# Two-operand head work on VectorE, score copies and a scale on ScalarE, and a later first weight load in a decoder trunk on one NeuronCore

## The chip, the core and the metric

The kernel runs on one core of a Trainium2 chip. A core has five engines with queues of their own: TensorE (PE, with a separate queue for weight loads, PEld), VectorE (DVE), ScalarE (ACT), GpSimd (POOL) and SyncE (SP), which here only issues DMAs. The metric is device time of one execution in microseconds, the median over runs; lower is better.

## The reference

One layer of a hybrid decoder on 1024 tokens of width 1024, with 16 learned tokens put in front, all in float32:

```
u = rmsnorm(h, mix_norm_pre)
q, f_logit, i_in, g_out, v_pool, gate_a, gate_b = split(u @ w_in)      # 512 x5, 1024 x2
a = hgrn2(q, f_logit, i_in, g_out, lb, out_norm)      # 4 heads of 128 x 128
p = multiscale_pool(v_pool, pool_proj, pool_scale)    # windows 2, 4, 8, 16
z = sigmoid(gate_a) * (a @ w_branch_hgrn) + sigmoid(gate_b) * (p @ w_branch_pool)
h = h + rmsnorm(z @ w_out, mix_norm_post)
u = rmsnorm(h, ffn_norm_pre)
y = (gelu(causal_dwconv(u @ ffn_w_gate)) * (u @ ffn_w_up)) @ ffn_w_down   # width 2816
h = h + rmsnorm(y, ffn_norm_post)
```

The part that the change works in is `hgrn2`, a linear recurrence with a decay per token and channel:

```
f     = lb + (1 - lb) * sigmoid(f_logit)
log_f = log(max(f, 1e-30))
k     = (1 - lb) * sigmoid(-f_logit)
state = exp(log_f) * state + k v^T ;  o = q state
o     = rmsnorm(o per head) * out_gain * sigmoid(g)
```

## The kernel before

*Stages.* The kernel goes once through these stages, with 128 channels on the partitions and all tokens along the free axis: norms of the input rows and the V projection (to about 80 us), the first output gates G0 and G1 and the branch gates (to about 260), the head stage (260 to 480), the two branch projections (480 to 560), the mixing with w_out (560 to 700), the FFN's gate and up projections (700 to 1115) and its down projection (to the end). Every weight tile is split for two-term arithmetic: ACT casts it to `whi`, and another engine subtracts, `wlo = wraw - whi` (L155).

*The start.* `load_row` loads one of nine tiles of input rows (L454). Their loads are written first, then four weight tiles (`wiraw`, L459) and small parameters (`prow`, L478). The first loads of the output gate's weights, `gl` (a `Loader`, whose `wsplit` has its load at L151), are written far later, inside the loop over V tiles. PE begins with warm-up matmuls (L507, `pj`) until the first normalised row is there to be transposed (L431, `pt<-ident,un`).

*The head stage.* The order of projections (F: forget gate, Q, G: output gate, PV and PP: pooling) and of the four heads' steps (`h0` to `h3`, `c0` to `c3`) is written out by hand in `ORDER`. After an F projection, `post_f` takes two sigmoids of it, `f` and `kk`, and `chain_f` (the `c` steps) makes from them the scaled `kk`, the logarithm of the decay in two pieces (`f2` and `f`, two ACT logarithms), their sum (L636) and its running sum `b` (L637). `head_steps` then makes the scores within chunks of 128 tokens in levels of 2, 4, 8, 16, 32 and 64 tokens. `level_in` makes for each level the differences `d` from `b` (L684), two exponentials on ACT (L686, L687), and the products with `q` (L688) and `kk` (L689). `level_mm` multiplies these on PE into a bank `sl` (L699 for the levels 32 and 64, L705 for the small ones). `level_out` brings the bank into `sc` by copies (L714, levels 32 and 64) or into `near` by masked copies (L720). Then come the decayed `kd` and `qs`, transposes of `kd` into `kt` (L763), the diagonal products of `kk` and `q` (`kk` scaled by `e1` at L755, matmuls L773 into `sb`, copies L777 into `sc`), the state (`ds`, L790), the output `o`, its square `rs` (L814), the split of that for a mean by matmul (L872, `rh`), and the norm (L821, L822). A projection's matmuls are L208 to L212, its banks `pg` for G, `pq` for Q.

*Who does what.* Names of operations such as `lq64.0` (level 64's product with `q`, head 0) go through this function:

```
    def eng(op):
        return pool_e if op in POOLED else dve
```

`POOLED` names 44 operations: 31 of the heads' two-operand operations (with one split of `rs`), and 13 (`w...`) subtractions of weight splits.

*What sets the order.* PE, ACT and DVE run in the written order at the start and in parts of the stages after it, under `tc.manual_schedule`; elsewhere the framework's scheduler orders each engine's instructions, by its own estimates and by when buffers come free. SP's DMAs are ordered by it everywhere.

Of the kernel before, what the change touches and what calls it, by code (L numbers as in the profile page):

```python
# [11 lines left out]
AF = mybir.ActivationFunctionType  # L12
ALU = mybir.AluOpType

P = 128
# [19 lines left out]
NCH = 8  # L35
# [4 lines left out]
LOG_FLOOR = 1e-30  # L40
LSPLIT = 2.0 ** -60
LUP = 2.0 ** 60
# [6 lines left out]
EARLY_G = 2  # L49
# [12 lines left out]
POOLED = ("e1k.0 e1k.3 kdmul.2 kdmul.3 kdsub.2 lk32.1 lk4.1 lq16.1 lq32.1 lq32.2 lq64.0 lq64.3 lq8.0 lq8.1 lq8.2 "  # L62
          "osg.2 sub2.2 sub32.1 sub8.1 wBA2 wBA6 wBA7 wBB2 wF0 wF2 wF3 wPP2 wPV0 wPV1 wQ0 wQ1 lq4.3 kdsub.1 qsmul.1 "
          "lk32.0 e1q.3 e1q.1 lq2.1 wQ2 sub2.3 rsl.0 lk32.3 lq64.1 qsmul.2").split()
TRUNC = False

CH_ALL = [(0, 348), (348, 346), (694, 346)]
# [4 lines left out]
def trunk_kernel(ctx: ExitStack, tc: tile.TileContext, x, meta_tokens, mix_norm_pre,  # L72
# [3 lines left out]
    nc = tc.nc  # L76
    act, dve, pool_e, pe = nc.scalar, nc.vector, nc.gpsimd, nc.tensor
# [24 lines left out]
    def slot(n, dtype=F32, name="s"):  # L102
        return stage["fm", "p"].tile([P, n], dtype, tag="fm", name=nm(name), padded_shape=[P, LP])
# [17 lines left out]
    def small(shape, name, tag, bufs=4):  # L121
        return sm.tile(shape, F32, tag=tag, name=nm(name), bufs=bufs)
# [328 lines left out]
    def load_row(t0, rows):  # L451
        row = slot(D, name="row")
        src = meta_tokens[:, :] if t0 == 0 else x[0, t0 - NM : t0 - NM + rows, :]
        nc.sync.dma_start(row[:rows], src)  # L454
        return row

    def load_wi(j):
        raw = slot(1024, name="wiraw")
        nc.sync.dma_start(raw.rearrange("p (k c) -> p k c", k=2), wblock(WIN, 2 * j, 2, CI, 512))  # L459
        return raw  # L460
# [24 lines left out]
    oml = const.tile([P, HEADS], F32, name="oml")  # L485
# [90 lines left out]
    SB = 32  # L576
# [39 lines left out]
    def eng(op):  # L616
        return pool_e if op in POOLED else dve

# [8 lines left out]

    def chain_f(h, kk, b, f, f2):
        dve.tensor_scalar(f, f, oml[:, h : h + 1], lb[:, h : h + 1], ALU.mult, ALU.add)
        dve.tensor_scalar(kk, kk, oml[:, h : h + 1], None, ALU.mult)  # L630
        dve.tensor_scalar(f2, f, LUP, 1.0, ALU.mult, ALU.min)
        dve.tensor_scalar(f2, f2, LOG_FLOOR * LUP, None, ALU.max)
        dve.tensor_scalar(f, f, LSPLIT, None, ALU.max)
        act.activation(f2, f2, AF.Ln)
        act.activation(f, f, AF.Ln)
        eng(f"lf.{h}").tensor_tensor(f, f, f2, ALU.add)  # L636
        dve.tensor_tensor_scan(b, keep_on, f, 0.0, ALU.mult, ALU.add)  # L637
        heads[h].update(kk=kk, b=b, f=f)
# [7 lines left out]
    def head_steps(h):  # L646
        q, kk, b, lf = (heads[h][z] for z in ("q", "kk", "b", "f"))
# [5 lines left out]
        sc = slot(NCH * P, name="sc")  # L653
        scm, em = small([NM, HALO], "scm", "scm", 2), small([P, HALO * NM], "em", "em", 2)
        near = small([P, NCH * SB], "near", "near", 2)
        n3 = near.rearrange("p (c t) -> p c t", c=NCH)
        pool_e.memset(sc, 0.0)
        pool_e.memset(near, 0.0)

        def over(t):  # L660
            return t[:, :NM].rearrange("p (o t) -> p o t", o=1).to_broadcast([P, HALO, NM])
# [46 lines left out]
        def level_out(lv, ps):  # L708
            if lv >= SB:
                o3 = sc.rearrange("p (c t) -> p c t", c=NCH)  # L710
                p3 = ps[:, : NCH * lv].rearrange("p (c h) -> p c h", c=NCH)
                for i in range(P // (2 * lv)):
                    n = 2 * lv * i
                    dve.tensor_copy(o3[n : n + lv, :, n + lv : n + 2 * lv], p3[n : n + lv])  # L714
                return
            o4 = near.rearrange("p (c b two h) -> p c b two h", c=NCH, two=2, h=lv)[:, :, :, 1, :]
            p4 = ps[:, : NCH * SB // 2].rearrange("p (c b h) -> p c b h", c=NCH, h=lv)
            nb = SB // (2 * lv)
            m4 = masks[lv].rearrange("p (o b h) -> p o b h", o=1, h=lv).to_broadcast([P, NCH, nb, lv])
            dve.copy_predicated(o4, m4, p4)  # L720
# [195 lines left out]
    def job(kind, i):  # L916
        if kind == "F":
            return (wblock(WIN, 0, KD, CF + i * P, P), KD, u_all, CH_ALL, lambda r: post_f(i, r))
        if kind == "Q":
            return (wblock(WIN, 0, KD, CQ + i * P, P), KD, u_q, CH_Q, lambda r: post_q(i, r))  # L920
        if kind == "G":
            return (wblock(WIN, 0, KD, CG + i * P, P), KD, u_q, CH_Q, lambda r: post_g(i, r))
        if kind == "PV":
            return (wblock(WIN, 0, KD, CV + i * P, P), KD, u_all, CH_ALL, lambda r: post_pv(i, r))
        if kind == "PP":
            return (pool_proj[0, i].rearrange("(k c) d -> c k d", k=1), 1,
                    lambda k, lo, n: (pin[i][0][:, lo : lo + n], pin[i][1][:, lo : lo + n]), CH_Q,
                    lambda r: post_pp(i, r))
        if kind == "BA":
            return (wblock(w_branch_hgrn[0], 0, HEADS, i * P, P), HEADS, a_x, CH_Q, lambda r: post_branch(sas, i, r))  # L930
        return (wblock(w_branch_pool[0], 0, HEADS, i * P, P), HEADS, p_x, CH_Q, lambda r: post_branch(sbs, i, r))
# [122 lines left out]
    with tc.manual_schedule(engines={E.Activation, E.DVE, E.PE}):  # L1054
        warm(14)
        n0, n1 = (norm_steps(rows_in[i], P, g1) for i in range(2))
        next(n0)
        next(n0)
        un0 = next(n0)
        f0 = feature_steps(un0, P, uhi, ulo, vtiles[0][0])  # L1060
        split_wi(raws[0])
        next(f0)
        next(f0)
        next(f0)
        next(n1)
        next(f0)
        next(n1)
        un1 = next(n1)
        v_mm(vb[0], vtiles[0][0], 0)
        v_mm(vb[0], vtiles[0][0], 1)  # L1070
        split_wi(raws[1])
        f1 = feature_steps(un1, P, uhi, ulo, vtiles[1][0])
        next(f1)
        next(f1)
        split_wi(raws[2])
        next(f1)
        next(f1)
        split_wi(raws[3])
        for i, j in ((0, 1), (1, 0), (0, 2), (1, 1), (0, 3), (1, 2), (1, 3)):
            for k in (2 * j, 2 * j + 1):  # L1080
                v_mm(vb[i], vtiles[i][0], k)
        v_norm(2)
        v_norm(3)
        for i in range(2):
            v_feat(2 + i)
            v_norm(4 + i)
        for i in range(2):
            v_out(vb[i], vtiles[i][0])
        for i in range(2, len(vtiles)):
            ps = bank("pv")  # L1090
            for k in range(KD):
                v_mm(ps, vtiles[i][0], k)
            if i < 5:
                v_feat(i + 2)
            if i == 5:
                v_feat(7)
                v_feat(8)
            v_norm(i + 4)
            if i == 3:
                params()  # L1100
            if i == 5:
                for q in ("t2", "t1", "t3", "t4"):
                    two_halves(gq, q)
                sums = [gate_steps(d) for d in ds]
            if i == len(vtiles) - 1:
                gl = Loader([job("G", h)[:2] + (P,) for h in range(EARLY_G)])
            for j in SUMS_AT.get(i, ()):
                next(sums[j], None)
            v_out(ps, vtiles[i][0])
        gates.load_first(0)  # L1110
        gates.load_first(1)
        gates.ahead(2)
        for h in range(EARLY_G):
            src, n_k, xs, chunks, post = job("G", h)
            r = proj(None, 0, n_k, xs, chunks, ws=gl.next(), name="pg", by_bank=2 * h)
            if h == EARLY_G - 1:
                post(r)
            for j in SUMS_AT.get(9 + 2 * h, ()):
                next(sums[j], None)
            if h < EARLY_G - 1:  # L1120
                post(r)
            if h == 0:
                dve.tensor_tensor(vm_hl[:NM], vm_hl[:NM], vm_low[:NM], ALU.add)
                nc.sync.dma_start(vmd, vm_hl[:NM])
                gates.load_first(2)
                gates.ahead(4)
            for j in SUMS_AT.get(10 + 2 * h, ()):
                next(sums[j], None)

        close_pool("ps")  # L1130
        open_pool("pf", 4, PSUM)
        gates.load_first(3)
        for e in range(0, EARLY, 2):
            p = gates.start_pair(e)
            for f in [f[i] for i in range(2) for f in p]:
                f()
                for j in SUMS_AT.get(13, ()) if e == 0 else ():
                    next(sums[j], None)
# [31 lines left out]
    for kind, i in order:  # L1170
# [18 lines left out]
        src, n_k, xs, chunks, post = job(kind, i)  # L1189
# [34 lines left out]
    for name, names in (("v1", ("b11h", "b11l", "b21h", "b21l")), ("v2", ("b22h", "b22l", "t1h", "t1l"))):  # L1224
        n, o = (HP, HO) if name == "v1" else (HN, 0)
# [113 lines left out]
    rows, z_at = {}, {}  # L1339
# [470 lines left out]
```

## Time and profile before

| | before |
|---|---|
| median of 3 runs | 1331.35 us (1329.1 to 1331.79) |
| the profiled execution's own time | 1331.5 us |
| its span | 1329.8 us |
| mean granted TensorE clock | 0.991 |
| PE busy | 1302.7 us, 98% |
| PEld busy | 1159.9 us, 87% |
| DVE busy | 968.0 us, 73% |
| ACT busy | 572.9 us, 43% |
| POOL busy | 438.5 us, 33% |
| DMA moved | 230.56 MB, 173 GB/s on average |

The span is the part of an execution that the profiler's records cover; the profiled execution's own time is 1.7 us longer. "Busy" counts the time in which an engine works on an instruction; "granted clock" is the share of full speed that TensorE was allowed. The records name instructions by line of the kernel (L154), by operation, and by output and inputs (`whi<-wraw`). Times are from one profiled execution.

### The profile page before, as it was taken

To read this page: it belongs to the slowest core of one execution; us is meant where nothing else is said; L and a number is where in the kernel's file an instruction comes from. 1 tells how busy PE (TensorE), PEld (TensorE's weight loads), DVE (VectorE), ACT (ScalarE), POOL (GpSimd) and SP (SyncE) were. 2 spreads that over 40 slices of the span, in tenths; PEclk is the share of its full clock that TensorE was granted. 3 is DMA by queue.
4 is the path that set the end of the run, shared out by engine and by line. 5 is a ranking of instruction groups with operands and counts; after the bars stand their busy time and mean duration, and the time that the engine had idled before them with its cause. 6 is when DMAs were issued, how large, how long until landed. Compare 5 with 4: busy or idle time off the path is not lost.

```text
span 1329.8 us, 21860 instructions
## 1 busy us (share of the span) xinstructions
PE 1302.7 (98%) x8665; PEld 1159.9 (87%) x8665; DVE 968.0 (73%) x1229; ACT 572.9 (43%) x962; POOL 438.5 (33%) x333
## 2 busy tenths in 40 slices
PE   8999999998899999999999999999999999999997
PEld 6799899998898999987899888888888888888886
DVE  5765655379967767766678999888999895455757
ACT  5553333366666665235564222322222233444443
POOL 2015331226624710051025555545555652000000
PEclk9999999998998999999999999999999999999999
DMA  7134533321011157987686777676766799666644
GB/s 260 53 105 145 134 111 104 108 69 49 19 52 36 35 175 263 337 287 253 229 291 231 192 207 193 196 206 164 181 157 141 183 237 318 216 224 222 222 174 158
DMA packets 139832, 230.56 MB, mean 173 GB/s; under 512 B 9080, under 2 KB 77340, under 8 KB 139730
## 3 DMA queue, kind: packets, MB, share of 16 engines
q1 hardware_dynamic: 127666, 204.78, 45.9%
q0 software_dynamic: 12064, 24.38, 11.1%
q8 instruction: 68, 1.11, 0.3%
q14 instruction: 34, 0.28, 0.1%
HBM read 165.59 MB, written 86.57 MB: 190 GB/s over the span
## 4 chain that ended last, share of the span: by engine, by line
PE 91%; DVE 3%; ACT 2%; DMA 2%; issue 1%; POOL 1%; SPq 0%; DVEq 0%; ACTq 0%
PE P L311 15%; PE P L312 15%; PE P L314 15%; PE pd L188 5%; PE pd L190 5%; PE pd L189 5%; PE pm L188 2%; PE pm L190 2%; PE pm L189 2%; PE ppv L208 1%; PE ppv L212 1%; PE ppv L209 1%; PE pbb L208 1%; PE pbb L209 1%; PE pbb L212 1%; PE pv L189 1%
## 5 line engine op out<-in xcount | busy, mean ns | idle before, releaser
L312 PE MATMUL P<-v,whi 128*128 128x512 f32 (+2 forms) x408 | 140.7, 353 | 0.0
L311 PE MATMUL P<-v,whi 128*128 128x512 f32 (+2 forms) x408 | 140.7, 352 | 0.0
L314 PE MATMUL P<-v,wlo 128*128 128x512 f32 (+2 forms) x424 | 135.1, 349 | 0.0
L1544 DVE TENSOR_TENSOR rot<-wraw,rot 128x1024 fp32r<-128x1024 f32 x31 | 37.9, 1224 | 72.3 <-ACT rot L1543 72.3
L282 POOL TENSOR_TENSOR swa<-wraw,wraw 128x512 f32<-128x512 f32 x28 | 43.4, 1549 | 138.9 <-DMA wraw<-in_ffn_w_gate_dram 73.9
L311 PEld LDWEIGHTS P<-v,whi 128*128 128x128 f32 x408 | 76.7, 188 | 10.5
L312 PEld LDWEIGHTS P<-v,whi 128*128 128x128 f32 x408 | 76.6, 188 | 10.2
L314 PEld LDWEIGHTS P<-v,wlo 128*128 128x128 f32 x424 | 74.0, 188 | 10.8
L256 ACT CAST whi<-wraw 128x512 fp32r<-128x512 f32 x78 | 46.1, 617 | 86.5 <-PE P L312 63.0
L190 PE MATMUL pd<-rot 128*128 128x512 f32 x272 | 82.1, 389 | 0.0
L189 PE MATMUL pd<-rot 128*128 128x512 f32 x272 | 82.1, 389 | 0.0
L188 PE MATMUL pd<-rot 128*128 128x512 f32 x272 | 81.1, 389 | 0.1
L1543 ACT CAST rot<-wraw 128x1024 fp32r<-128x1024 f32 x31 | 32.7, 1054 | 90.8 <-PE pd L190 89.4
L257 DVE TENSOR_TENSOR wlo<-wraw,whi 128x512 fp32r<-128x512 f32 x74 | 65.9, 912 | 2.8 <-ACT whi L256 2.7
L256 ACT CAST whi<-swa 128x512 fp32r<-128x512 f32 x56 | 33.4, 619 | 79.2 <-PE P L312 76.4
L1472 DVE SCALAR_TENSOR_TENSOR y<-g,par,y 128x1024 f32<-128x1024 f32 x44 | 65.6, 1491 | 0.8
L257 DVE TENSOR_TENSOR wlo<-swb,whi 128x512 fp32r<-128x512 f32 x56 | 61.4, 1102 | 6.0 <-ACT whi L256 6.0
L256 ACT CAST whi<-swb 128x512 fp32r<-128x512 f32 x56 | 33.4, 619 | 69.8 <-PE P L312 65.4
L188 PEld LDWEIGHTS pd<-rot 128*128 128x128 f32 x272 | 51.1, 188 | 11.1 <-DVE p L1480 0.5
L189 PEld LDWEIGHTS pd<-rot 128*128 128x128 f32 x272 | 51.0, 188 | 10.6
L190 PEld LDWEIGHTS pd<-rot 128*128 128x128 f32 x272 | 51.0, 188 | 10.6
L311 PE MATMUL P<-t4h,whi 128*128 128x258 f32 (+1 forms) x196 | 57.0, 307 | 0.0
(426 smaller groups left out, 4096.0 us busy)
## 6 DMA issues: line engine op xcount, KB each, us to landing
wraw<-in_w_in_dram SPq DMA_DIRECT2D x36, 512.0 KB, 5.1
yt<-ysum SPq DMA_DIRECT2D x33, 512.0 KB, 5.4
wraw<-in_ffn_w_gate_dram SPq DMA_DIRECT2D x26, 512.0 KB, 6.4
wraw<-in_ffn_w_up_dram SPq DMA_DIRECT2D x22, 512.0 KB, 5.9
wsum<-in_ffn_w_down_dram SPq DMA_DIRECT2D x22, 512.0 KB, 9.1
wraw<-in_w_out_dram SPq DMA_DIRECT2D x18, 512.0 KB, 4.8
ysum<-ys SPq DMA_DIRECT2D x11, 768.0 KB, 6.8
sa<-sscr SPq DMA_DIRECT2D x16, 513.0 KB, 6.4
```

What stands on the lines that cost most here:

```text
L188: pe.matmul(ps, ahi, bhi, start=first, stop=False)
L189: pe.matmul(ps, ahi, blo, start=False, stop=False)
L190: pe.matmul(ps, alo, bhi, start=False, stop=last)
L256: act.copy(hi, src)
L257: (pool_e if 4 <= i < 2 * self.early else dve).tensor_tensor(lo, src, rr(hi), ALU.subtract)
L282: pool_e.tensor_tensor(s1, a21, a22, ALU.add)
L311: pe.matmul(d, whi[:, k, :], xh[:, c : c + w], start=(k == 0 and onto is None), stop=False, **go)
L312: pe.matmul(d, whi[:, k, :], xl[:, c : c + w], start=False, stop=False, **go)
L314: pe.matmul(x[:, o : o + w], wlo[:, k, :], xh[:, c : c + w], start=False, stop=(k == 3), **go)
L1472: dve.scalar_tensor_tensor(a, g[:, j : j + SEQ], cvw[:, j, m : m + 1], a, ALU.mult, ALU.add)
L1543: act.copy(hi, src)
L1544: dve.tensor_tensor(lo, src, rr(hi), ALU.subtract)
```

## The change

It has six edits.

- `POOLED` is empty: all the operations that it named run on DVE. POOL keeps the setting-up of tiles and the pooling sums (L855).
- In `chain_f` the scale of `kk` by `oml` moves from DVE to ACT.
- In `chain_f` the two clamps of `f2` become one, and the factor LUP moves into the logarithm's own scale. The clamp takes the logarithm's argument from LOG_FLOOR up to LSPLIT where it was 1/LUP; `f` is clamped from below by LSPLIT as it was.
- `near` is set to zero by a copy from the zeroed `sc`, on POOL, where it was a second memset on POOL.
- In `level_out` the copies into `sc` (L714) move from DVE to ACT.
- The `Loader` of the first output gate is built under `tc.issue_after` of the last row's load, so that its DMAs stand behind the row loads in SP's queue.

```diff
-POOLED = ("e1k.0 e1k.3 kdmul.2 kdmul.3 kdsub.2 lk32.1 lk4.1 lq16.1 lq32.1 lq32.2 lq64.0 lq64.3 lq8.0 lq8.1 lq8.2 "
-          "osg.2 sub2.2 sub32.1 sub8.1 wBA2 wBA6 wBA7 wBB2 wF0 wF2 wF3 wPP2 wPV0 wPV1 wQ0 wQ1 lq4.3 kdsub.1 qsmul.1 "
-          "lk32.0 e1q.3 e1q.1 lq2.1 wQ2 sub2.3 rsl.0 lk32.3 lq64.1 qsmul.2").split()
+POOLED = ()
...
-        nc.sync.dma_start(row[:rows], src)
+        loaded_row.append(nc.sync.dma_start(row[:rows], src))
         return row
+
+    loaded_row = []
...
     def chain_f(h, kk, b, f, f2):
         dve.tensor_scalar(f, f, oml[:, h : h + 1], lb[:, h : h + 1], ALU.mult, ALU.add)
-        dve.tensor_scalar(kk, kk, oml[:, h : h + 1], None, ALU.mult)
-        dve.tensor_scalar(f2, f, LUP, 1.0, ALU.mult, ALU.min)
-        dve.tensor_scalar(f2, f2, LOG_FLOOR * LUP, None, ALU.max)
+        act.activation(kk, kk, AF.Copy, scale=oml[:, h : h + 1])
+        dve.tensor_scalar(f2, f, LOG_FLOOR, LSPLIT, ALU.max, ALU.min)
         dve.tensor_scalar(f, f, LSPLIT, None, ALU.max)
-        act.activation(f2, f2, AF.Ln)
+        act.activation(f2, f2, AF.Ln, scale=LUP)
         act.activation(f, f, AF.Ln)
...
         pool_e.memset(sc, 0.0)
-        pool_e.memset(near, 0.0)
+        pool_e.tensor_copy(near, sc[:, : NCH * SB])
...
                 for i in range(P // (2 * lv)):
                     n = 2 * lv * i
-                    dve.tensor_copy(o3[n : n + lv, :, n + lv : n + 2 * lv], p3[n : n + lv])
+                    act.copy(o3[n : n + lv, :, n + lv : n + 2 * lv], p3[n : n + lv])
                 return
...
             if i == len(vtiles) - 1:
-                gl = Loader([job("G", h)[:2] + (P,) for h in range(EARLY_G)])
+                with tc.issue_after(loaded_row[-1].ins):
+                    gl = Loader([job("G", h)[:2] + (P,) for h in range(EARLY_G)])
```

What this does to the order of instructions is shown at three places. In the changed kernel lines 62 to 455 have a number lower by two than before, and lines 633 to 1105 a number lower by one.

The first place is SP's queue at the start of the program. `row` is a tile of input rows, `wraw_737` the first weights of G0. Before:

```order
L1805 UNCONDITIONAL_BRANCH
L151 DMA wraw_737<-in_w_in_dram 128x8x128
L454 DMA row_90<-in_x_dram 128x1024
L145 DMA g_8_92<-in_mix_norm_pre_dram 128x1024
L459 DMA wiraw_94<-in_w_in_dram 128x2x512
L454 DMA row_96<-in_x_dram 128x1024
```

After, the same stretch, and the queue again behind the last row's load:

```order
L1805 UNCONDITIONAL_BRANCH
L452 DMA row_90<-in_x_dram 128x1024
L143 DMA g_8_92<-in_mix_norm_pre_dram 128x1024
L459 DMA wiraw_94<-in_w_in_dram 128x2x512
L452 DMA row_96<-in_x_dram 128x1024
```

```order
L452 DMA row_116<-in_x_dram 128x1024
L478 DMA prow_118<-in_ffn_conv_w_dram 66x128
L478 DMA prow_118<-in_ffn_conv_b_dram 22x128
L478 DMA prow_118<-in_hgrn_lower_bounds_dram 4x128
L478 DMA prow_118<-in_hgrn_out_norm_dram 4x128
L478 DMA prow_118<-in_pool_scale_dram 4x128
L149 DMA wraw_737<-in_w_in_dram 128x8x128
L149 DMA wraw_743<-in_w_in_dram 128x8x128
```

The load of `wraw_737` has moved from ahead of the first row to behind the last row and the parameters.

The second place is DVE's queue in the head stage, around the levels 32 and 64 of head 0 (`d_3124`, `d_3130` before, `d_3122`, `d_3128` after) and 2 and 4 of head 1 (the other two). Before:

```order
L684 TENSOR_TENSOR d_3124<-b_2632 128x1024
L684 TENSOR_TENSOR d_3130<-b_2632 128x1024
L155 TENSOR_TENSOR wlo_3023<-wraw_3020,whi_3022 128x1024
L720 COPY_PREDICATED near_2742<-mask_159,sl_3030 128x16x8
L689 TENSOR_TENSOR d_3074<-d_3074,kk_2842 128x256x2
L688 TENSOR_TENSOR d_3080<-d_3080,q_3026 128x128x4
L688 TENSOR_TENSOR d_3124<-d_3124,q_2731 128x16x32
L720 COPY_PREDICATED near_2742<-mask_166,sl_3090 128x8x16
L689 TENSOR_TENSOR d_3130<-d_3130,kk_2631 128x8x64
L684 TENSOR_TENSOR d_3305<-b_2843 128x1024
L720 COPY_PREDICATED near_3071<-mask_145,sl_3231 128x64x2
L720 COPY_PREDICATED near_3071<-mask_152,sl_3265 128x32x4
```

After:

```order
L683 TENSOR_TENSOR d_3128<-b_2632 128x1024
L153 TENSOR_TENSOR wlo_3021<-wraw_3018,whi_3020 128x1024
L719 COPY_PREDICATED near_2741<-mask_159,sl_3028 128x16x8
L687 TENSOR_TENSOR d_3072<-d_3072,q_3024 128x256x2
L688 TENSOR_TENSOR d_3072<-d_3072,kk_2841 128x256x2
L687 TENSOR_TENSOR d_3078<-d_3078,q_3024 128x128x4
L688 TENSOR_TENSOR d_3078<-d_3078,kk_2841 128x128x4
L687 TENSOR_TENSOR d_3122<-d_3122,q_2730 128x16x32
L688 TENSOR_TENSOR d_3122<-d_3122,kk_2631 128x16x32
L687 TENSOR_TENSOR d_3128<-d_3128,q_2730 128x8x64
L719 COPY_PREDICATED near_2741<-mask_166,sl_3088 128x8x16
L688 TENSOR_TENSOR d_3128<-d_3128,kk_2631 128x8x64
```

The products of `d` with `q` and `kk` that were missing from DVE's queue (those of level 2 with `q`, level 4 with `kk`, level 32 with `kk`, level 64 with `q`) now stand in it, and all eight come one after the other.

The third place is ACT's queue around the output gate G3, late in the head stage. `pt` is the bank that the transposes write and L763 (L762 after) frees, `ms` that of the squares' mean. Before:

```order
L814 ACTIVATE rs_5018<-o_5017 128x1026
L767 COPY ktm_5062<-pt_5060 16x128
L872 CAST rh_5043<-rs_5018 128x1026
L777 COPY sc_4274<-near_4277 32x8x32 x4
L154 CAST whi_5124<-wraw_5122 128x128
L763 COPY kt_5047<-pt_5048 128x512
L763 COPY kt_5047<-pt_5054 128x512
L821 ACT_TABLE_LOAD
L821 ACTIVATE rs_4297<-ms_5136,eps_t 128x342
```

After:

```order
L766 COPY ktm_5058<-pt_5056 16x128
L813 ACTIVATE rs_5014<-o_5013 128x1026
L776 COPY sc_4270<-near_4273 32x8x32 x4
L871 CAST rh_5039<-rs_5014 128x1026
L152 CAST whi_5120<-wraw_5118 128x128
L820 ACT_TABLE_LOAD
L820 ACTIVATE rs_4293<-ms_5132,eps_t 128x342
L820 ACTIVATE rs_4293<-ms_5136,eps_t 128x342
L820 ACTIVATE rs_4293<-ms_5140,eps_t 128x342
L762 COPY kt_5043<-pt_5044 128x512
L762 COPY kt_5043<-pt_5050 128x512
```

The four copies into `sc` (L777 before, L776 after) and the cast `rh` have changed places, and the two copies into `kt`, which stood ahead of the table load, now stand behind it and the three logarithms.

## The prediction

> **What bounds the kernel now.** I read first the page's span and its chain of work that ended last, then the list of waits of PE (TensorE), then the stretches of 20 us.
>
> ```profile
> span 1329.8 us, 21860 instructions
> ...
> PE 91%; DVE 3%; ACT 2%; DMA 2%; issue 1%; POOL 1%; SPq 0%; DVEq 0%; ACTq 0%
> ```
>
> Nine tenths of the end time is matmuls one behind the other. An edit off PE pays only where PE stood still, so the next view is PE's waits (engine, line, releaser: total us, times, longest):
>
> ```profile
> PE sl L705 <- issue: 2.7, 1, 2.7
> PE sb L773 <- POOL kk L755: 2.5, 1, 2.5
> PE sl L699 <- DVE d L689: 2.1, 1, 2.1
> PE sl L699 <- DVE d L688: 1.7, 1, 1.7
> ...
> PE pg L208 <- ACT kt L763: 1.3, 1, 1.3
> PE ds L790 <- DVE sc L714: 1.0, 1, 1.0
> ```
>
> All of these lie in the head stage (about 260 to 480 us). Its stretches (span, then busy us of PE, PEld, DVE, ACT, POOL, then granted clock, DMA share, GB/s) show the engine behind them:
>
> ```profile
> 300.00:320.00 20.00, 16.16 (x247) 15.61 (x246) 19.90 (x15) 13.59 (x23) 17.00 (x9) 0.83 0.27 79
> 320.00:340.00 20.00, 20.00 (x249) 19.76 (x248) 18.40 (x19) 11.38 (x17) 10.62 (x5) 1.00 0.03 7
> 340.00:360.00 20.00, 16.50 (x258) 15.43 (x257) 18.02 (x21) 12.92 (x22) 12.88 (x9) 0.91 0.09 27
> ```
>
> VectorE (DVE) is busy 56.3 of these 60 us and GpSimd (POOL) 40.5; PE loses 7.3 us and a part of its clock. ScalarE (ACT) has 22 us free.
>
> **Part 1, the first load.** The chain begins so (start, us, what):
>
> ```profile
> 0.81 0.44 SPq L151
> ...
> 1.30 5.53 DMA row<-in_x_dram
> ```
>
> SyncE first issues the G0 weights (L151, 512 KB), then row 0. Moved rates by the microsecond from 0:
>
> ```profile
> GB/s 0 11 202 170 325 418 375 383 422 410 397 389 385 397 410 422 410 393 414 283 348 400 263 285 265 277 69 0 0 0 0 0 39 381 105 0 0 109 154 0
> ```
>
> The first 0.52 MB are through at about 4.4 us, the second at about 5.8, and row 0 lands at 6.83. Without G0 ahead the row is issued 0.49 us earlier and has 0.52 MB less before it. That is worth 1.3 us at the peak rate of 418 GB/s and 2.7 us at the rates of those first microseconds. What follows on ACT, DVE and PE up to the first transpose is a chain of single steps and moves with the row, but PE has its own floor:
>
> ```profile
> 2.03 5.26 PE L507 MATMUL pj<-ident,onesm 128*128 128x128 f32 x28 [2.03 <-POOL ident masks.py:199]
> 9.46 0.87 PE L431 MATMUL pt<-ident,un 128*128 128x128 f32 x3 [2.17 <-DVE un L420]
> ```
>
> The warm-up matmuls hold PE until 7.29, so no more than the 2.17 us it waits there can be won. I take 2.2, as the nearer bound of the rate is above it; bounds 1.3 and 2.2. G0's own load now lands before 30 us and is used after 50: nothing. PE has no wait from 20 to 280 us, so the shift stays.
>
> **Part 2, two-operand work from POOL to DVE.** Of POOL's work in 300 to 360 us these are the first and last of 17 tensor operations:
>
> ```profile
> 300.58 2.27 POOL L688 TENSOR_TENSOR d<-d,q 128x512 f32<-128x512 f32 x1 [9.94 <-ACT d L686]
> ...
> 355.70 2.04 POOL L754 TENSOR_TENSOR q<-q,e 128x512 f32<-128x512 f32 x1
> ```
>
> On DVE, with POOL idle, the same kinds cost:
>
> ```profile
> 274.49 2.35 DVE L684 TENSOR_TENSOR d<-b 128x1024 f32<-128x1024 f32 x2
> ...
> 276.99 0.69 DVE L688 TENSOR_TENSOR d<-d,q 128x512 f32<-128x512 f32 x1
> ...
> 277.59 0.69 DVE L689 TENSOR_TENSOR d<-d,kk 128x512 f32<-128x512 f32 x1
> ```
>
> That is 0.6 us from start to start for 512 columns, 1.2 for 1024. The 17 are eleven of 512 and six of 1024 or two pieces: 6.6 + 7.2 = 13.8 us more for DVE in these 60. That would not fit, but DVE's own work there is stretched:
>
> ```profile
> 297.96 5.97 DVE L684 TENSOR_TENSOR d<-b 128x1024 f32<-128x1024 f32 x4
> ...
> 307.79 4.19 DVE L688 TENSOR_TENSOR d<-d,q 128x512 f32<-128x512 f32 x2
> ...
> 312.09 2.63 DVE L689 TENSOR_TENSOR d<-d,kk 128x512 f32<-128x512 f32 x1
> ```
>
> ```profile
> 308.98 2.45 POOL L684 TENSOR_TENSOR d<-b 128x1024 f32<-128x1024 f32 x1
> ```
>
> Two operations of 0.6 took 4.19 us while POOL ran; the next took 2.63. What a two-operand operation lasts on POOL (2.3), DVE largely stands, so moving it to DVE costs 0.6 and frees more.
>
> *Place B, h0's levels 32 and 64.* PE there:
>
> ```profile
> 308.90 1.54 PE L705 MATMUL sl<-d 128*32 128x16 f32 x125
> 312.12 0.70 PE L699 MATMUL sl<-d 128*32 128x32 f32 x32 [1.68 <-DVE d L688]
> 314.87 1.94 PE L699 MATMUL sl<-d 128*64 128x64 f32 x16 [2.06 <-DVE d L689]
> 316.74 0.66 PE L208 MATMUL pq<-uhi,whi 128*128 128x342 f32 x1
> ```
>
> In the new order DVE has, from 298.0: four L684 (4.6), one weight split (1.2), eight products (4.8), two mask copies (0.4): done at 309.0, and 0.7 later for the scale that now runs on ACT ahead of the logarithms. PE comes at 310.4, so both waits go. PE would reach the pq matmuls at 312.1 instead of 316.7: 4.6 us. The clock of 0.83 also goes with the waits: the half-rate period after 316.7 lasts to 320.0 (3.3 us), which costs 1.7. B: 6.3 us won (bounds 3.8, the idle time alone, and 6.3).
>
> *Place C, kk times e1 of head 0.* The chain, and ACT's prices:
>
> ```profile
> 326.03 1.06 ACT f L635
> 327.11 1.25 DVE f L636
> 328.39 2.32 DVE b L637
> ...
> 344.07 1.71 POOL kk L755
> 345.82 0.76 PE sb L773 x50
> ```
>
> ```profile
> 463.93 1.64 ACT L777 COPY sc<-near 32x256 f32<-32x256 f32 x4
> 465.60 0.30 ACT L154 CAST whi<-wraw 128x128 fp32r<-128x128 f32 x1
> 465.80 1.07 ACT L763 COPY kt<-pt 128x512 f32<-128x512 f32 x2
> 466.88 1.28 ACT L821 ACT_TABLE_LOAD   x1
> 468.18 1.43 ACT L821 ACTIVATE rs<-ms,eps_t 128x342 f32<-128x342 f32 x3
> ```
>
> F2's matmuls end as before. ACT's six sigmoids, table load and four exponentials end at 316.5 now that the differences are there; then come the scale of kk (1.0, as L635), the three score copies (two of 0.4 as L777, one of 0.6 as L763), a table load of 1.3 and two logarithms (2.0): 322.2 instead of 327.1. On DVE the addition and scan (3.6) and then 14.1 us of undisturbed work (six of 1024 as L684 at 1.2, a weight split of 1.2, seven of 512 at 0.6, five small ones) bring kk to 339.9 instead of 345.8: 5.9 earlier. PE comes 6.3 earlier, so the wait L773 <- kk stays, with DVE in POOL's place, and grows by about 0.4. The stretch after it had a clock of 0.91, half rate for some 3.5 us; a longer wait may double that, so I charge 0.8 more. C: 1.2 lost (bounds 0 and 2.1).
>
> *Place D.* The score copy L714 leaves the full DVE queue for ACT, which is free: its wait of 1.0 goes (bounds 0 and 1.0).
>
> *Place F, the G3 gate.* In ACT's new order the four copies L777 stand ahead of the cast L872, and the table load and three L821 stand ahead of the kt copies L763, which free PSUM banks. PE's next projection waits for such a bank:
>
> ```profile
> 466.43 0.42 PE L208 MATMUL pg<-uhi,whi 128*128 128x342 f32 x1 [1.32 <-ACT kt L763]
> ```
>
> After the last cast (start 465.6, 0.2 until the next) a table load of 1.3 and one L821 of 0.5 end at about 467.6, plus 0.3 for the transposes that now stand between the output matmuls: PE starts near 467.9, 1.5 later. If the bank is that of the first kt copy, three L821 and a copy come first: 2.9 later. I take 1.5, since L821 now frees its banks first. Such a wait of 2.8 us is as long as that at L773, so half a clock period (1.7) is charged: 3.2 lost (bounds 1.5 and 6.3).
>
> **Part 3, the rest.** The clamp (L632) and the scale (L630) leave DVE, 0.7 each and head, already counted in C. The near copy replaces a memset on POOL, which is now nearly idle: nothing, and if it were late, one mask copy would wait 0.3. Weight splits F0 to Q2 move to DVE where it is half idle. The `issue` wait of 2.7 (in the middle of 64 equal matmuls, with no engine to wait for) is untouched. The DMA-heavy stage after 480 us starts earlier with the heads and keeps its order.
>
> **Sum.** -2.2 - 6.3 + 1.2 - 1.0 + 3.2 = -5.1. The profiled execution's own time is 1331.5 (span 1329.8 and 1.7 around it): 1326.4. The median of the runs, 1331.35, lies 0.15 below that execution, which puts it at 1326.3.
>
> **Rivals.**
> - *The late bank.* ACT's order at F costs its upper bound, 6.3, and the first load only 1.3: -1.3 - 6.3 + 1.2 - 1.0 + 6.3 = -1.1, 1330.3, no measurable change. For it: L763 is what PE waits for now. Against: two other banks come free earlier. It decides from 1.4 us of further wait.
> - *DVE becomes the bound (the other side).* If DVE's long operations have another cause than POOL, the 13.8 us land on an engine with 3.7 us free: 10.1 more on C's chain, -2.2 + 10.1 = +7.9: 1339.3. It decides where a moved product of 512 columns costs over 1.5 us instead of 0.6. Against it: 0.69 us rows whenever POOL is idle.
> - *The waits at F and `issue` fade.* PE's stream shifts against its other engines, F costs nothing and the `issue` wait does not recur: -9.5 + 1.2 - 2.7 = -11.0, 1320.4. Nothing in the order removes them.
> - *The clock stays up.* If waits of under 3 us leave the clock at full rate, the 0.8 of C and the 1.7 of F fall away: 1323.8. Against it: 0.91 in 340 to 360 after a wait of 2.5 us. The Trainium skill, "TensorE: Matmul & The Clock Gate", section "HAM oscillation — how this bites in real kernels", gives the rule "no PE-idle gaps >~3.4µs", by which waits of this length would be free and the sum 1323.8; the stretch's clock of 0.91 speaks against it.
>
> **How the numbers follow.** The forecast has 0.44, the clock 0.10, fading 0.10, the late bank 0.26, DVE as bound 0.10. A measurement of this kernel tells about 0.2% (2.7 us) from no change, so faster is under 1328.7: the first three, 0.64; same 0.26; slower 0.10. The range runs from the fading case with C at its lower bound (1320.4 - 1.2 = 1319.2) to the late bank with C and D at their upper ones (1330.3 + 0.9 + 1.0 = 1332.2); it leaves out DVE as bound and the far ends of these two.
>
> **What would show it.** Right: the row's transfer at the head of the chain ends near 4.5 us and L431 starts near 7.3; no wait of L699 on DVE; products L688 at 0.69 throughout; POOL under 1 us in most of 300 to 360; a wait of L773 on DVE kk of about 3 us; PE's wait before pg of about 3 us, released by ACT. Wrong: DVE still at 18 us or more of 20 between 300 and 360, a new wait of L705 or L208 on ACT in the head stage, or PE waiting for ACT's L714.

## The result and the profile after

| | before | after |
|---|---|---|
| median | 1331.35 us (5 runs, 1328.56 to 1331.99) | 1324.72 us (5 runs, 1321.43 to 1326.72) |
| ratio to before | | 0.9950, 95% interval 0.9936 to 0.9965 |
| the profiled execution's own time | 1331.5 us | 1326.72 us |
| its span | 1329.8 us | 1325.0 us |
| POOL busy | 438.5 us | 355.5 us |
| DVE busy | 968.0 us | 948.7 us |

The change makes the kernel 0.5% faster, 6.6 us by the medians. The profiled execution is the slowest of its five, so the traces show 4.8 us of that.

DVE has 22 instructions more after the change and is busy 19 us less. PE's waits in the changed kernel (engine, line, releaser: total us, times, longest):

```profile
PE pg L206 <- ACT rs L820: 3.4, 1, 3.4
PE sl L704 <- issue: 2.7, 1, 2.7
PE sb L772 <- DVE kk L754: 2.3, 1, 2.3
...
PE sl L698 <- DVE near L719: 1.1, 1, 1.1
PE pt L429 <- DVE un L418: 1.1, 2, 0.8
```

The two waits of L699 for `d` and that of the state (`ds`) for a score copy are gone. The wait for kk has DVE for its releaser now, the wait before G3 (`pg`) has grown from 1.3 to 3.4 and is put down to the logarithms, and L698 has a new wait of 1.1 for a masked copy. The same three stretches of the head stage as before (span, busy us of PE, PEld, DVE, ACT, POOL, then clock, DMA share, GB/s):

```profile
300.00:320.00 20.00, 19.88 (x285) 19.03 (x284) 15.94 (x26) 16.17 (x27) 0.00 (x0) 1.00 0.29 81
320.00:340.00 20.00, 16.61 (x294) 15.96 (x294) 19.74 (x28) 16.96 (x27) 0.96 (x1) 0.96 0.10 28
340.00:360.00 20.00, 20.00 (x341) 19.05 (x341) 13.86 (x24) 9.71 (x19) 0.40 (x1) 0.87 0.02 5
```

In 300 to 320 DVE does 26 instructions in 15.94 us where it did 15 in 19.90; PE is full and the clock 1.00. The loss has moved to 335 to 340, and the half clock after it to 340 to 345. DVE's groups in 300 to 318 (line, operation, shapes, count | busy us, mean ns | idle before):

```profile
L683 DVE TENSOR_TENSOR d<-b 128x1024 f32<-128x1024 f32 x4 | 4.7, 1218 | 0.0
L687 DVE TENSOR_TENSOR d<-d,q 128x512 f32<-128x512 f32 x6 | 4.1, 685 | 1.0 <-ACT d L685 1.0
L688 DVE TENSOR_TENSOR d<-d,kk 128x512 f32<-128x512 f32 x6 | 4.1, 684 | 0.0
```

Every product takes 0.68 us; before, two of them had taken 4.19 between them. To see where PE's time came from, the start of each matmul after is compared with the start of the same matmul before. The shift of PE's stream goes like this:

| up to | shift, us | step |
|---|---|---|
| 20 us | -1.96 | -1.96, the first load |
| 323 us | -7.74 | -5.78, place B |
| 356 us | -5.94 | +1.80, place C |
| 360 us | -7.21 | -1.27, place D |
| 462 us | -8.08 | -0.87, between |
| 470 us | -4.39 | +3.69, place F |
| end | -4.77 | -0.38, the branch stage |

From 566 us to the end the shift stays within 0.1 us.

### The profile page after: what moved, and what is told of

Same layout as the page of the kernel before. It is cut to its first block, busy times and chain, and to the rows that moved or that the text cites. A ratio compares the mean times of both kernels' runs of the same rounds, so it can differ in the third digit from the quotient of the medians.

```text
span 1325.0 us, 21836 instructions
## 1 busy us (share of the span) xinstructions
PE 1302.5 (98%) x8665; PEld 1158.7 (87%) x8665; DVE 948.7 (72%) x1251; ACT 581.0 (44%) x978; POOL 355.5 (27%) x291
## 4 chain that ended last, share of the span: by engine, by line
PE 92%; DMA 3%; ACT 2%; DVE 1%; issue 1%; SPq 0%; DVEq 0%; ACTq 0%
PE P L309 15%; PE P L310 15%; PE P L312 15%; PE pd L186 5%; PE pd L187 5%; PE pd L188 5%; PE pm L186 2%; PE pm L187 2%; PE pm L188 2%; PE pf L206 1%; PE ppv L206 1%; PE pf L207 1%; PE ppv L210 1%; PE ppv L207 1%; PE pg L206 1%; PE pq L210 1%
```

## The experiments

Each kernel was timed beside the kernel before on its chip. The ratio to before is what is compared from one chip to another.

| kernel | median, us | before there | ratio, 95% interval |
|---|---|---|---|
| the change | 1324.72 | 1331.35 | 0.9950 (0.9936 to 0.9965) |
| the change, a second time | 1323.89 | 1329.86 | 0.9953 (0.9941 to 0.9966) |
| first load ahead again | 1327.95 | 1330.1 | 0.9981 (0.9970 to 0.9992) |
| the list on POOL again | 1329.96 | 1330.1 | 0.9994 (0.9982 to 1.0006) |
| scale and copies on DVE again | 1325.32 | 1330.1 | 0.9959 (0.9944 to 0.9974) |
| twins on POOL, thin | 1326.95 | 1329.53 | 0.9977 (0.9966 to 0.9989) |
| twins on POOL, wide | 1348.99 | 1329.53 | 1.0139 (1.0122 to 1.0156) |
| kt copies first | 1322.36 | 1329.53 | 0.9943 (0.9929 to 0.9957) |
| wide warm-up | 1322.82 | 1329.53 | 0.9949 (0.9935 to 0.9963) |
| kt first and wide warm-up | 1321.72 | 1329.86 | 0.9934 (0.9922 to 0.9947) |
| these, one product on POOL | 1322.09 | 1329.86 | 0.9936 (0.9922 to 0.9949) |
| steps swapped, wide warm-up | 1318.29 | 1329.86 | 0.9910 (0.9897 to 0.9924) |

### The parts of the change

**The first load ahead again.** `gl` is built without `issue_after`.

> The changed kernel with the first output gate's load back ahead of row 0 in SP's queue, nothing else. Theory (the row waits for that transfer): PE's first transpose is about 2 us later and the shift is carried to the end, so +2.0 against the changed kernel, about 1326.7; the row's load again ends near 6.8 us. Rival (the start is set by PE's warm-up matmuls or by the parameters behind the rows): no change, about 1324.7.

The chain of work that ended last up to 9 us, and PE's first transpose:

```profile
1.31 5.72 DMA row<-in_x_dram
```

```profile
9.65 1.94 PE L429 MATMUL pt<-ident,un 128*128 128x128 f32 x8 [2.58 <-DVE un L418]
```

The row lands at 7.0 and PE's stream is 2.1 us later than in the changed kernel up to 400 us, which is the theory's figure, and 1.5 later at the end. The ratio says 0.31 points, about 4 us, more than the trace, but the two intervals nearly touch.

**The list on POOL again.** `POOLED` as before the change, all else of the change kept.

> The changed kernel with the 44 operations back on POOL; the scale and the score copies stay on ACT, the single clamp and the late first load stay. Theory (POOL's operations stretch DVE's, and that makes the waits of the head stage): DVE is again at 18 us or more of 20 around 300 to 360, L698 waits for d again, and the 5 us won in the head stage go: about 1329. Rival (the moves to ACT carry the gain): at most 1 us lost, about 1325.5.

No gain is left: the interval of the ratio reaches over 1. PE's waits and DVE's groups in 300 to 320 in this kernel:

```profile
PE sl L700 <- DVE d L690: 2.1, 1, 2.1
...
PE sl L700 <- DVE d L689: 1.7, 1, 1.7
```

```profile
L690 DVE TENSOR_TENSOR d<-d,kk 128x512 f32<-128x512 f32 x3 | 6.6, 2216 | 0.0
L685 DVE TENSOR_TENSOR d<-b 128x1024 f32<-128x1024 f32 x3 | 4.9, 1666 | 0.0
L689 DVE TENSOR_TENSOR d<-d,q 128x512 f32<-128x512 f32 x2 | 4.2, 2130 | 0.0
```

Both waits of place B are back with their old lengths, and DVE's own products take 2.1 to 2.2 us again. PE is 6.8 us behind the changed kernel at 318 us. At the end of the two profiles it is only 2.0 behind, because some of the change's own losses are absent here: PE does not wait for kk, and its wait before `pg` is 1.3, for a kt copy, as in the kernel before. So the longer wait at `pg` comes with the emptied list and not with the moves to ACT. The loss of about 6 us is that of the ratios; the change's profile is of the slowest of its five runs, and this one's lies 1.2 us below its median.

**Scale and copies on DVE again.**

```diff
-        act.activation(kk, kk, AF.Copy, scale=oml[:, h : h + 1])
+        dve.tensor_scalar(kk, kk, oml[:, h : h + 1], None, ALU.mult)
...
-                    act.copy(o3[n : n + lv, :, n + lv : n + 2 * lv], p3[n : n + lv])
+                    dve.tensor_copy(o3[n : n + lv, :, n + lv : n + 2 * lv], p3[n : n + lv])
```

> The changed kernel with the scale of kk and the copies L713 back on DVE. Theory (with POOL quiet DVE has room, ACT only takes a small part): DVE gets 0.7 more per head for the scale and 0.3 to 0.6 for each copy, the wait at kk grows by 1 to 2 us and a wait for a score copy may return: 1325.7 to 1327. Rival (taking work off DVE matters as much as POOL): 4 us or more, 1329.

The ratio cannot be told from the change's. PE waits 2.9 us at `sb` in place of 2.3, but L698's new wait is not there, and the stream is 1.2 us ahead of the changed kernel's profiled run at the end. The moves to ACT bought nothing measurable, although DVE is busy for all of the 20 us from 320 to 340 here. The score-copy wait of place D does not return here either, with the copy on DVE.

The single clamp and the copy that zeroes `near` were not run alone. By the ratios the three parts come to 0.84 points where the change gains 0.50; the intervals are too wide to tell whether the parts simply add up.

### Contention or latency

That the list on POOL costs 6 us does not say how. Its products of 512 columns last 1.3 to 2.3 us there in place of 0.69, and they may also slow DVE. So DVE keeps all of them, and POOL does some a second time for nobody. These are 29 (the expectations say 41; the splits and one gate product were left without a twin):

```diff
+    def twin(op, t, at=0, n=1024):
+        if op in TWIN:
+            for _ in range(n // 512):
+                pool_e.tensor_tensor(scr, t[:, at : at + 512], t[:, at + 512 : at + 1024], ALU.mult)
...
             eng(f"lk{lv}.{h}").tensor_tensor(db[:, :, 0, :], db[:, :, 0, :], blocks(kk, lo, lv)[:, :, 0, :], ALU.mult)
+            twin(f"lq{lv}.{h}", d, NM, 512)
+            twin(f"lk{lv}.{h}", d, NM, 512)
```

A first version had the twin of each product with `q` ahead of the product with `kk`, which writes the tile that the twin reads.

> The changed kernel (all operations on DVE), with 41 of those that POOL had before done a second time on POOL, into a scratch tile that nobody reads, at about the same time. It costs one tile of the main pool and some changes of order. Theory (contention: a two-operand operation on DVE lasts as long as POOL's beside it): DVE's products of 512 columns take about 2 us again where a twin runs, DVE is full from 300 to 360, and the time rises by 5 us or more, to 1330 or above. Rival (latency: what cost time before was only that an operation in the chain took 2.3 us on POOL in place of 0.7 on DVE): products stay at 0.69, about 1325.

It took 1351.72 us (ratio 1.0160, 1.0142 to 1.0178), but DVE sat idle for POOL's reads (three waits, 6.1 us together, in the head stage), which is neither theory. The second version, as above, and its thin partner leave DVE nothing to wait for in the stretch that is read below:

> The changed kernel with 41 of the operations that POOL had before done a second time there, 512 columns wide, into a scratch tile that nobody reads; nothing else waits for them but the release of tiles. Theory (contention): DVE's products of 512 columns last about 2 us where a twin runs beside them, DVE is at 18 us or more of 20 between 300 and 360, the waits of L698 for d (by its number here) come back: 4 us or more above twin_thin. Rival (latency of the moved operations in the chain): products stay at 0.69 us and the time is within 1 us of twin_thin.

> The same program as twin_wide with the twins 8 columns wide, so that POOL works next to nothing. DVE's order is that of twin_wide up to late in the head stage. It carries the cost of the scratch tile and of the changed order alone; both theories expect products of 0.69 us and a time between 1325 and 1330.

DVE's groups from 308 to 319, thin first, then wide:

```profile
L691 DVE TENSOR_TENSOR d<-b 128x1024 f32<-128x1024 f32 x2 | 2.4, 1216 | 0.0
L697 DVE TENSOR_TENSOR d<-d,kk 128x512 f32<-128x512 f32 x3 | 2.0, 680 | 0.0
...
L637 DVE TENSOR_SCALAR f<-f,oml,lb 128x1040 f32<-128x1040 f32 x1 | 0.8, 791 | 0.0
```

```profile
L691 DVE TENSOR_TENSOR d<-b 128x1024 f32<-128x1024 f32 x2 | 4.6, 2328 | 0.0
...
L697 DVE TENSOR_TENSOR d<-d,kk 128x512 f32<-128x512 f32 x1 | 1.6, 1608 | 0.0
L637 DVE TENSOR_SCALAR f<-f,oml,lb 128x1040 f32<-128x1040 f32 x1 | 1.6, 1574 | 0.0
```

The last columns say that DVE is idle for nobody: the instructions themselves last 1.1 us longer for 1024 columns, 0.9 for 512, 0.8 for a one-operand operation of 1040. The whole kernel is 22 us above the thin one, whose own ratio is 0.27 points above the change's; what the scratch tile and what the order has of that is not separated. In both kernels DVE does 1251 instructions, and it is busy for 985.5 us in the wide one against 950.5. Contention is shown; no operation of the chain ran on POOL. The 22 is more than the list ever cost, as is to be expected where DVE carries the operations as well; late in the head stage the two kernels also differ in order, but in the profiles 12.8 us are already lost by 360. How the 6 us of the list divide in the kernel before is not measured: the products that PE waited for at place B were DVE's own, stretched, while kk at place C was POOL's, so that latency can have had a part there.

The Trainium skill, "SBUF — State Buffer", section "SBUF: two separate sides", says that VectorE and GpSimd share one pair of ports as an exclusive lock, for a VectorE operation in a two-port mode or, against a GpSimd operation that reads SBUF, with two SBUF inputs; the loser waits for a whole instruction. The thin kernel agrees from the other side, in POOL's group from 308 to 319:

```profile
L625 POOL TENSOR_TENSOR scr<-b 128x8 f32<-128x8 f32 x2 | 2.1, 1063 | 0.2
```

A POOL operation on 8 columns lasts 1.06 us beside DVE's 1024 columns. In the same trace it lasts 0.20 us where DVE stands still (at 394.64 and 426.67, for example), so 0.86 of the 1.06 is waiting for its turn.

### The waits that are left

**The kt copies first.** An ordering edge puts the two copies of head 3 into `kt` ahead of head 0's three logarithms; PE's and DVE's orders stay.

```diff
-            act.activation(rs[:, lo : lo + n], ps[:, :n], AF.Ln, bias=eps_t)
+            with tc.issue_after(kt_copy[3 if h == 0 else h].ins):
+                act.activation(rs[:, lo : lo + n], ps[:, :n], AF.Ln, bias=eps_t)
```

> The changed kernel with the two kt copies of head 3 ordered ahead of the three logarithms L820 of head 0 on ACT; no other engine's order changes. Theory (PE's projection pg waits for any bank, and the table load and the logarithm stand in front of it): the copies start near 458.5 and free a bank at 459.1 in place of 460.4, so the wait shrinks by 1.3 us and the time is 1323 to 1324. Rival (the bank that pg gets is one of those that the logarithms free): the logarithms come 1.1 us later, and so does PE: 1326.

ACT in the changed kernel, then in this one (start, us):

```profile
457.28 1.05 ACT L871 CAST rh<-rs 128x1026 fp32r<-128x1026 f32 x1
458.23 0.29 ACT L152 CAST whi<-wraw 128x128 fp32r<-128x128 f32 x1
458.54 1.28 ACT L820 ACT_TABLE_LOAD   x1
459.84 1.42 ACT L820 ACTIVATE rs<-ms,eps_t 128x342 f32<-128x342 f32 x3
461.13 0.59 ACT L762 COPY kt<-pt 128x512 f32<-128x512 f32 x1
```

```profile
458.55 1.07 ACT L762 COPY kt<-pt 128x512 f32<-128x512 f32 x2
459.63 1.28 ACT L821 ACT_TABLE_LOAD   x1
```

PE's wait at `pg` is 2.0 in place of 3.4 and is released by the copy, so a bank that the copy frees serves as well as one that a logarithm frees. Against the second run of the change PE gains 2.9 us across this place, half-clock time included. In this profile it had lost 2.5 ahead of it, at the `issue` wait (2.7 here, 1.8 there) and after it, and it loses 0.5 more in the branch stage, so the spans are equal, 1321.2 both, and the ratio cannot be told from the change's.

**The wide warm-up.**

```diff
-            pe.matmul(junk_bank[:, :P], onesm, ident, start=True, stop=True)
+            pe.matmul(junk_bank.rearrange("p (o n) -> p o n", o=4), onesm,
+                      ident.rearrange("p (o n) -> p o n", o=1).to_broadcast([P, 4, P]), start=True, stop=True)
...
-        warm(14)
+        warm(3)
```

> The changed kernel with the 14 warm-up matmuls of 128 columns replaced by 3 of 512, so that every later instruction of PE stands some 40 places earlier in its stream; all else stays. Theory (the wait named issue, 2.7 us in the middle of 64 equal matmuls, is PE waiting for the next block of its instructions, since an instruction transfer ends just before PE goes on): the boundary falls among longer matmuls and the wait goes, with the half clock after it: 3 to 4.5 us less, about 1321. Rival (the wait belongs to those matmuls, whatever their place in the stream): it stays at the same line and the time at 1324.7. A third way: the boundary of another block falls among short matmuls, and a wait appears elsewhere.

The place of the `issue` wait in the changed kernel (second run), and in this one, with ACT's cast:

```profile
399.44 0.60 PE L704 MATMUL sl<-d 128*32 128x16 f32 x48
401.80 0.32 PE L704 MATMUL sl<-d 128*32 128x16 f32 x16 [1.75 <-issue]
402.05 0.74 PE L818 MATMUL ms<-rh,onesr 128*128 128x342 f32 x3
```

```profile
398.82 0.74 PE L705 MATMUL sl<-d 128*32 128x16 f32 x64
401.11 0.74 PE L819 MATMUL ms<-rh,onesr 128*128 128x342 f32 x3 [1.55 <-ACT rh L872]
```

```profile
400.02 1.04 ACT L872 CAST rh<-rs 128x1026 fp32r<-128x1026 f32 x1
```

The 64 matmuls run through, so the wait hung on their place in the stream and not on them. But the next matmuls need `rh`, whose cast ends at 401.06: 1.55 us of a real wait had stood behind the wait named `issue`. PE gains 0.3 us here against that run, and 2.8 against the first profile, whose wait was 2.7 with half clock after it. The ratio cannot be told from the change's: the theory was right that the wait is one of place, and too high on the price.

**Both edits, and one product back on POOL.** All four of these ran on one chip, the change among them.

> The changed kernel unaltered, so that the three beside it can be compared with it on one chip. Every theory expects its ratio to the kernel before between 0.9936 and 0.9965; its waits at kk, at pg and the one named issue recur at the same places.

> The changed kernel with two edits of the runs before: the kt copies of head 3 ahead of the three logarithms on ACT, and the 3 wide warm-up matmuls. Theory (two separate waits of PE, 1.4 us of one and 2.7 of the other, with parts of a half-clock period each): the gains add up, 4 to 6 us under the changed kernel, about 1319.5 on the first chip. Rival (what is won ahead of 557 us is given back at the wait for the branch weights, L162 to L208): no more than 2 us.

The two together are 2.2 us under the change, with no run of the one within the range of the other (1320.60 to 1322.35, and 1322.89 to 1324.80): between the theory and the rival. The rival has something to it. In the two profiles PE is 2.6 us ahead at 500 us but only 0.5 at the end, since it waits in the branch stage for `whi` (0.9) and `sa` (0.7), which it does not in the change's second profile; those profiles are of the slowest run of the one and the fastest of the other.

```diff
-POOLED = ()
+POOLED = ("e1k.0",)
```

> The kernel with both edits and one product on POOL, that of head 0's kk with e1, for which PE waits 2.3 us. Theory (on DVE it stands behind twelve others; POOL can take it as soon as kd is made, near 331, and needs 1.6 to 3 us, while DVE loses 1.1): the wait for kk goes, that for near's masked copy grows by about 1, net 1 to 2.5 us under the kernel with both. Rival (any POOL work beside a full DVE costs more than it saves): 0 to 2 us above it.

```profile
330.78 2.23 POOL L755 TENSOR_TENSOR kk<-kk,e 128x512 f32<-128x512 f32 x1 [8.46 <-DVE kd L746]
```

```profile
PE sl L699 <- DVE near L720: 4.0, 1, 4.0
```

POOL has kk ready at 333.0 and the wait of 2.2 for it is gone. But the masked copy that L699 waits for follows on the same DVE queue, and that wait is 4.0 instead of 1.2. The copy even ends 0.3 us later (340.04 against 339.74), with one product fewer ahead of it, because DVE paid for POOL's product:

```profile
331.75 1.31 DVE L668 TENSOR_TENSOR em<-em,kk 128x32 f32<-128x32 f32 x1
```

This operation on 32 columns takes 0.18 us in the kernel with both edits. The medians differ by 0.4, within the noise. DVE sets the end of that place whoever makes kk.

**The steps swapped.** Head 3's transposes are written ahead of head 2's output, with the wide warm-up.

```diff
-"sp1 PVb3 h2 h3 h3 sp3 PP1 h0 G3
+"sp1 PVb3 h3 h2 h3 sp3 PP1 h0 G3
```

> The changed kernel with the 3 wide warm-up matmuls and, in the order of steps, head 3's transposes written ahead of head 2's output. The kt copies then stand right behind ACT's copies of the output, ahead of the square and the casts. Theory (pg waits for the first free bank of any kind): a bank is free before the means are through, the wait before pg goes wholly, 3.4 us, with the half clock after it: 1 to 3 us under the kernel with both. Rival (the bank that pg gets is given out by the scheduler ahead of time and belongs to the means): the wait stays at 3 us or more, and the square that is 1.2 us later adds to it.

```profile
450.70 1.07 ACT L763 COPY kt<-pt 128x512 f32<-128x512 f32 x2 [3.60 <-PE po L810]
451.66 0.18 ACT L804 COPY o<-po 128x2 f32<-128x2 f32 x1
```

The copies are through before PE reaches `pg`, and PE's list of waits begins with these, without one at `pg`:

```profile
PE sb L773 <- DVE kk L755: 2.2, 1, 2.2
PE ms L819 <- ACT rh L872: 1.5, 1, 1.5
```

PE's stream gains 4.7 us against the kernel with both edits from 451 to 514 us, of which 3.8 are won by 480, at `pg` and by the half clock that follows it there, and 0.9 in the branch stage, where the wait for `sa` is gone. The time is 1318.29: 3.4 us under that kernel, a little more than the theory's 1 to 3, 5.6 under the change on the same chip, 11.6 under the kernel before. This is the fastest version of the study. The swap was not run without the wide warm-up.

## Why the prediction was right, point by point

The forecast was 1326.3 and a gain of 5.1; the medians give 6.6, and the profiled execution, at 1326.72, 4.8. That the total is so near is in part luck: the five places of the sum gave 3.5 in the trace, not 5.1, and the other 1.25 came where the sum had nothing.

- **The first load**, -2.2 forecast, -1.96 in the trace. The row was used from 4.30 as forecast, but the normalisation then waits for the gain behind it in the queue, which the sum did not have. PE starts its transposes at 7.98, not 7.3, which is 1.5 us earlier than before. The rest of the 1.96 is won by 20 us, a stretch whose granted clock was 0.91 before and is 1.00 after. The rows of the start:

```profile
4.30 1.06 ACT L413 ACTIVATE un<-row 128x1024 f32<-128x1024 f32 x1 [2.00 <-DMA row<-in_x_dram]
...
6.63 1.86 DVE L418 SCALAR_TENSOR_TENSOR un<-row,rstd,g 128x512 f32<-128x512 f32 x2 [0.66 <-DMA g<-in_mix_norm_pre_dram]
...
7.98 1.23 PE L429 MATMUL pt<-ident,un 128*128 128x128 f32 x8 [0.30 <-DVE un L418]
```

- **Place B**, -6.3 forecast, -5.78 measured. Both waits and the half clock went. That POOL's operations stretch DVE's, as the forecast read it from the rows, the twins show.
- **Place C**, +1.2 forecast, +1.80 measured, with other parts. The wait for kk did not grow (2.3 against 2.5): the logarithms ended at 320.2, not 322.2, because the exponentials ahead of them ended 2 us earlier than forecast, at 314.5. What came is a second wait right behind it, of L698 for a masked copy that stands in DVE's queue behind kk and three products, and half clock for twice as long. So the size is near the forecast, but not by its account:

```profile
337.03 0.69 DVE L754 TENSOR_TENSOR kk<-kk,e 128x512 f32<-128x512 f32 x1
...
339.45 0.29 DVE L719 COPY_PREDICATED near<-mask,sl 128x128 f32<-128x128 uint8 x1
...
339.79 1.07 PE L698 MATMUL sl<-d 128*32 128x32 f32 x32 [1.13 <-DVE near L719]
```

- **Place D**, -1.0 forecast, -1.27 measured. The stated reason, the copy's move to ACT, was not needed for it, as the run with the copies back on DVE shows.
- **Place F**, +3.2 forecast, +3.69 measured, by the mechanism named: logarithms and their table load ahead of the copies. The late-bank rival is refuted, since the first logarithm frees the bank, at 460.4. What the forecast had too low is ACT's lag: the last cast starts 1.2 us after PE has nothing left to do (458.23 against 457.0), where 0.5 was taken over from the profile before.
- **Costed at nothing**: the `issue` wait came back at its place, which refutes the fading rival for the changed kernel. That the clock stays up is refuted too: 0.87 after waits of 2.3 and 1.1.
- **VectorE as the bound**: 15.94 us of 20 where it had been 19.90, and no product above 0.7 in 300 to 318. The point from which this rival decides, 1.5 us for a product, was not come near to. But one sign that the prediction had named for being wrong did show in one of the three stretches: from 320 to 340 DVE is busy 19.74 of 20 us, and both of PE's waits at place C are for it. There DVE is the bound by the amount of its work, at undisturbed speed.

Between D and F lie 0.9 us that the sum did not have. The half-clock time after the `issue` wait was 6.8 us in the profile before and 3.4 in the profile after. Where such periods fall, and for how long, differs between profiles: behind the two waits of place C the change has a clock of 0.87 in 340 to 360, and the kernel with both edits, with the same two waits, 0.91; behind the `issue` wait the change has 3.4 us of half clock in one profile and none in the other. The change's own runs spread over 5.3 us, so a sum of this kind is not to be trusted below 1 or 2 us.

## What to carry to other kernels

An operation moved from VectorE to GpSimd to unload it can cost VectorE more time than it took there (here 1.13 us of stretching for a product that takes 0.60): look for rows of one shape that last two or three times as long while the other engine is busy, before counting what each engine has to do. When a wait is taken away, ask which other dependency ends next at that instruction: here a wait for instructions hid a wait for a cast, and a wait for one product hid one for a masked copy on the same queue. Where PSUM banks are shared by all users, the order of the copies that free them sets when a projection starts.

## What the runs showed of the hardware that was not expected

- PE can stand still in a run of short matmuls with no engine to wait for. The wait was 1.75 us in one profile of the changed kernel and 2.7 in another, in the middle of 64 equal matmuls. In the latter the trace has a 0.95 us transfer on the instruction queue from 400.35, and PE goes on at 402.62, that is 1.3 us after its end; in the kernel before it is 1.5. The Trainium skill, "Runtime: NRT & Kernel Launch", section "Instruction fetch mechanics", calls the cost of crossing a block of instructions "mostly hidden"; among matmuls of 342 columns no run showed such a wait, so that agrees there, and here it did not hold. That PE waited for the instructions of this transfer is the likeliest reading and not shown; what the shift of the stream shows is that the place in the stream decides.
- POOL's memset of 1024 columns (0.96 us at 323.73 in the thin twin kernel) did not stretch the DVE operation beside it, which took 1.22 us as ever.
